# Band attention values: from half-bank pieces spread over the head pairs to full-bank products at the band's entry, with a spill

## The chip, the cores and the metric

The kernel runs on one core of a Trainium2 chip. The metric is the device time of one execution in microseconds (us), here the median of several. TensorE (PE) multiplies matrices; its weight loads (PEld) overlap its matmuls. VectorE (DVE), ScalarE (ACT) and GpSimd (POOL) work elementwise; SyncE (SP) issues the transfers between the chip's DRAM and its on-chip memory, in the order of its queue. Matmul results land in PSUM, in banks of 128 x 512 f32.

## The reference, cut to what matters

The network has two layers, each a mixer and a SwiGLU feed-forward, over 1024 tokens and 1024 channels. The change touches the second mixer, chunked band attention with 16 heads of 64:

```python
def chunk_band_mixer(u, w_qkv, rel_bias, w_out):
    qkv = (u @ w_qkv).reshape(bsz, n_chunks, CHUNK, 3, C_HEADS, C_DIM)
    q, k, v = qkv[:, :, :, 0], qkv[:, :, :, 1], qkv[:, :, :, 2]
    ...
    scores = scores + bias.astype(jnp.float32)[None, None]
    p = jax.nn.softmax(jnp.where(valid[None, :, None, None, :], scores, -jnp.inf), axis=-1).astype(v.dtype)
    parts = [jnp.einsum('bnqhk,bnkhd->bnqhd', p[..., i * CHUNK:(i + 1) * CHUNK], v_p[:, i:i + n_chunks])
             for i in range(LEFT_CHUNKS + 1)]
    o = functools.reduce(jnp.add, parts)
    return o.reshape(bsz, seq, MIX_ODD) @ w_out
```

The values v are `u` (1024 x 1024) times the last 1024 columns of `w_qkv`. Each token attends to its own chunk of 64 and the eight before it.

## The kernel before

**Numbers.** An f32 operand is split into a rounded part (hi) and the rest (lo), and each product takes three matmuls, hi*hi, hi*lo, lo*hi (`mm3`, L286: lines 289, 290, 291). A weight tile of 128 x 512 is loaded into a buffer "wr"; a cast makes "wh" (L252 on ScalarE or L254 on VectorE), a subtraction makes "wl" (L257). There are four buffers of each kind.

**Memory.** Most tiles of 128 x 512 come from one heap of 60 units ("u", `unit`, L186). In the band, the normalized input takes 32 of them (two token halves x eight depth tiles x hi and lo) and the two rows of roots two more. PSUM is dealt out as "mm" (two banks, for projections and values), "z" (two pairs of banks, for scores, maxes and denominators) and "o" (two banks, for outputs).

**Order.** The framework's planner places the instructions on the engines: it goes by the order in which the program issues them, but where the next one isn't ready by its own estimates it takes a later one that is. On the chip each engine then keeps the order it was given. The feed-forward parts are pinned to program order; the band is not.

**The band** (`mixer1`, L1309). Heads go in eight pairs of 128 columns. At the entry come the values of pairs 0 and 1 (`vgen(0, [0, 1])`, L1319), the queries and keys of pair 0 (`band_project`, L1143) and the row maxes of its first token half. Then for each pair p, `weave` (L798) issues attention steps and, between them, work for the next pair in proportion to given costs: the projection of pair p+1 (2 weights x 2 halves x 8 depth tiles x 3 = 96 matmuls of 512 columns) and, for p < 6, the values of group p // 2 + 1 (two pairs, 256 columns) for token half p % 2. So the values' weights of the later groups are loaded and split twice, once for each half. Pair 6 has half of pair 7's projection as filler, and pair 7 the other half and the output projection.

`values` (L811) computes for each block of 128 tokens, with the input block as the stationary operand and 256 weight columns as the moving one; two blocks share a PSUM bank. `put_values` (L830) scales 128 x 128 pieces out of PSUM into units (L838).

An attention step (`band_attend`, L1198) is: scores into z (L1214, L1215), bias add on VectorE (L1216), exponential on ScalarE (L1217), running sum of exponentials on GpSimd (L1085), and some steps later the weighted sum of values (`weighted`, L840, line 844), four steps' sums issued together. `band_max` (L1174) computes scores (L1188), adds the bias and takes row maxes (L1191), and transposes them through TensorE (L1046) once for each pair and token half. `soft_finish` (L1097) makes the denominators (L1101) and stores the output tile (L1113). In `band_project`, L1152 scales the projection, L252, L257 and L1161 split it into units.

Of the kernel before, what the change touches and what calls it, by code (L numbers as in the profile page):

```python
# [10 lines left out]
F32 = mybir.dt.float32  # L11
F32R = mybir.dt.float32r
# [4 lines left out]
P = 128  # L17
S = 1024
D = 1024
KD = D // P  # L20
HALF = 512
# [137 lines left out]
class Trunk:  # L159
# [651 lines left out]
    def values(self, wsrc, s, kper, nk, ng, vts, hfs):  # L811
# [6 lines left out]
        for b0 in range(4 * hfs[0], 4 * hfs[-1] + 4, per):  # L818
# [8 lines left out]
                    yield 3 * MM_US * ncol / HALF  # L827
            self.put_values(s, ps, b0, ncol, vts)

    def put_values(self, s, ps, b0, ncol, vts):  # L830

        for g in range(ncol // P):
            if b0 % 4 == 0:
                vts[g].append(self.unit(F32, (P, 4, P)))
            for b in range(b0, b0 + HALF // ncol):
                hf, r = divmod(b, 4)
                v, q = vts[g][hf][:, r, :], ps[:, (b - b0) * ncol + g * P:][:, :P]
                self.nc.scalar.activation(v, q, AF.Identity, scale=s.rc[hf][:, r:r + 1])  # L838
# [470 lines left out]
    def mixer1(self, u, h_d, h2_d):  # L1309
        a = self.a  # L1310
        o_d = self.spill("o1_")
        out = Stream()
        half = lambda hf, *e: self.out_half(hf, a["w_out1"], o_p[hf], lambda hf, m: h_d[hf][m], list(range(KD)), out,
                                            h2_d, *e)
        with self.phase("band", BAND_TEMPS):
            vts = [[] for _ in range(8)]
            vgen = lambda g, hf: self.values([a["w_v1"][2 * g], a["w_v1"][2 * g + 1]], u, 4, KD, 1,
                                             vts[2 * g:2 * g + 2], hf)
            self.now(vgen(0, [0, 1]))  # L1319
            new = lambda: ([[], []], [[], []])  # L1320
            proj = new()
            self.now(self.band_project(0, u, proj))
            tq, tk = self.band_bias(0, "bias_q"), self.band_bias(0, "bias_k")
            self.now(self.band_max(0, proj, tq))
            for p in range(8):
                nxt, fill, cost, tqn, tkn = new(), iter(()), 0.0, None, None
                if p < 6:
                    fill = self.chain(self.band_project(p + 1, u, nxt), vgen(p // 2 + 1, [p % 2]))
                    cost = 28.0
                elif p == 6:  # L1330
                    fill, cost = self.band_project(7, u, nxt, [0]), 16.0

                def late(p=p, nxt=nxt):
                    nonlocal tqn, tkn
                    tqn, tkn = self.band_bias(p + 1, "bias_q"), self.band_bias(p + 1, "bias_k")
                    yield from self.band_max(0, nxt, tqn)

                first, second = (self.band_attend(p, hf, proj, tk, vts[p], o_d) for hf in range(2))
                top = self.band_max(1, proj, tq)
                if p < 7:  # L1340
                    self.weave(self.chain(self.with_max(first, top, 1), self.with_max(second, late(), 4)), 6.8,
                               fill, cost)
                else:
                    o_p = [[None] * KD, [None] * KD]
                    first = self.with_max(first, self.out_loads(o_d[0], 7, o_p[0]), 0)
                    second = self.with_max(second, self.out_loads(o_d[1], 7, o_p[1]), 0)
                    fill = self.chain(self.band_project(7, u, proj, [1]), self.free(top))
                    self.weave(self.ending(first), 2.5, fill, 8.0)
                    o_p[0][7] = o_d[0][7]
                    self.weave(self.ending(second), 5.0, half(0), 41.5)  # L1350
                    o_p[1][7] = o_d[1][7]
                proj, tq, tk = nxt, tqn, tkn
        return out, half(1, 1)
# [53 lines left out]
def _ktiles(w, cols):  # L1407
    w = w[:, cols]
    kt = w.shape[0] // P
    return np.ascontiguousarray(w.reshape(kt, P, w.shape[1]).transpose(1, 0, 2)).reshape(P, -1)  # L1410


def _mtiles(w, m=P):
    return np.stack([_ktiles(w, np.arange(i, i + m)) for i in range(0, w.shape[1], m)])


def _layout(i):
    out = {}
# [4 lines left out]
    w = i["ev_w_in"][0]  # L1423
    c = [np.arange(t * P, t * P + P) for t in range(5)]
# [6 lines left out]
    vt = []  # L1431
    for g in range(2):
        t = _ktiles(w, vb + np.arange(g * 256, g * 256 + 256))
        vt += [t[:, :1024], t[:, 1024:]]
    out["w_vb"] = np.ascontiguousarray(np.stack(vt))
    w = i["ev_w_uq"][0]
    uq = []
    for h in range(8):
        b = 96 * h
# [3 lines left out]
    w = i["ev_w_ukv"][0]  # L1443
# [4 lines left out]
    w = i["od_w_qkv"][0]  # L1448
    out["w_qk1"] = np.stack([_ktiles(w, o + np.arange(p * P, p * P + P)) for p in range(8) for o in (0, 1024)])
    vt = []  # L1450
    for g in range(4):
        t = _ktiles(w, 2048 + np.arange(g * 256, g * 256 + 256))
        vt += [t[:, :1024], t[:, 1024:]]
    out["w_v1"] = np.ascontiguousarray(np.stack(vt))
    out["w_out1"] = _mtiles(i["od_w_out"][0])
    out["w_gate"] = np.stack([_mtiles(i["w_gate"][l]) for l in range(2)])
# [1 line left out]
    w = np.stack([_mtiles(i["w_down"][l]) for l in range(2)])  # L1458
# [4 lines left out]
    w = w.reshape(w.shape[:3] + (FT, P))[:, :, :, order]  # L1463
    out["w_down"] = np.ascontiguousarray(w).reshape(w.shape[:3] + (FT * P,))
    rb = i["od_rel_bias"][0]
    s = np.arange(P)[:, None]
# [36 lines left out]
```

## Time and profile before

| what | value |
|---|---|
| times of three runs | 2551.01, 2552.98, 2554.29 us |
| median | 2552.98 us |
| profiled execution, its time | 2553.58 us |
| its span, first to last instruction | 2551.9 us |
| mean granted TensorE clock | 0.995 |
| values' evictions (L838) in the band | 64, from 1332.8 to 1717.5 us |
| band's score and max work | about 1373 to 1840 us |

A busy row counts the union of an engine's instructions. Matmuls overlap in a pipeline, so that one's duration is longer than the distance from its start to the next one's; the distance is what a stream costs. A row of windows gives the length, then busy time and count of each engine, the granted clock, the share of the DMA engines and GB/s. A row of groups gives line, engine, operation, tiles, shapes and count, then busy time and mean ns, then idle time before and what ended it. A row of waits gives who waited for whom, total, times and longest. A row of the timeline gives start and duration.

### The profile page before, as it was taken

The numbers are of one execution on the slowest core, as the hardware profiler recorded it, in microseconds if no ns is written. First come the engines' busy times: TensorE is split into PE (matmuls) and PEld (weight loads), VectorE is DVE, ScalarE is ACT, GpSimd is POOL, SyncE is SP. The second block draws the span as 40 slices with busy tenths as digits, with TensorE's granted clock in tenths as the row PEclk, the third lists the DMA queues.
The fourth block names the chain that finished last, engine by engine and source line by source line (L and its number), as shares of the span: only waits on it lengthen the run. The fifth ranks groups of instructions, "written<-read, shape, count | busy, mean of one in ns | idle before, by whom it ended". The sixth has DMA issues, their size and how long they took to land.

```text
span 2551.9 us, 33625 instructions
## 1 busy us (share of the span) xinstructions
PE 2478.1 (97%) x11710; PEld 1938.4 (76%) x11710; DVE 1858.1 (73%) x3072; ACT 1152.1 (45%) x1996; POOL 493.8 (19%) x475
## 2 busy tenths in 40 slices
PE   9999989999999999999999999999999999999997
PEld 7776766557778888888888777776777888888886
DVE  7988796565886666677766777777788676667775
ACT  5777565344454434433353443334445443443324
POOL 0333335652000000000031334345200000000004
PEclk9999999999999999999999999999999999999998
DMA  5222102125434334476652222223633433447661
GB/s 155 54 65 64 41 26 60 54 84 165 153 124 149 120 128 145 149 259 211 227 167 69 79 87 75 75 93 98 190 128 128 148 130 118 145 156 261 217 208 71
DMA packets 182250, 323.91 MB, mean 127 GB/s; under 512 B 21312, under 2 KB 37568, under 8 KB 182080
## 3 DMA queue, kind: packets, MB, share of 16 engines
q1 hardware_dynamic: 182080, 321.76, 38.0%
q8 instruction: 93, 1.52, 0.2%
q14 instruction: 77, 0.63, 0.1%
HBM read 222.58 MB, written 84.41 MB: 120 GB/s over the span
## 4 chain that ended last, share of the span: by engine, by line
PE 74%; DVE 8%; DMA 1%; ACT 1%; issue 1%; POOL 0%; DVEq 0%; SPq 0%; ACTq 0%; POOLq 0%
PE z L76 25%; PE mm L76 13%; PE o L76 7%; PE mm L289 6%; PE mm L290 6%; PE mm L291 6%; PE o L844 4%; DVE u L76 2%; PE z L1214 1%; PE z L1188 1%; PE z L1215 1%; PE z L1133 1%; DVE u L312 1%; PE z L1101 1%; PE z L1134 1%
## 5 line engine op out<-in xcount | busy, mean ns | idle before, releaser
L76 PE MATMUL z<-u,wh 128*128 128x512 f32 x976 | 302.3, 390 | 6.5 <-DVE u L76 6.5
L76 PE MATMUL z<-u,vh 128*128 128x512 f32 x976 | 301.8, 390 | 2.8 <-DVE u L76 2.8
L289 PE MATMUL mm<-u,wh 128*128 128x512 f32 x720 | 287.8, 400 | 3.5 <-DVE f L1003 1.4
L290 PE MATMUL mm<-u,wh 128*128 128x512 f32 x720 | 283.8, 394 | 0.0
L291 PE MATMUL mm<-u,wl 128*128 128x512 f32 x720 | 282.4, 393 | 0.0
L257 POOL TENSOR_TENSOR wl<-wr,wh 128x512 fp32r<-128x512 f32 (+2 forms) x95 | 122.0, 1289 | 803.3 <-ACT wh L252 736.0
L76 PE MATMUL mm<-u,wh 128*128 128x512 f32 x720 | 223.4, 392 | 4.6 <-ACT wh L76 4.6
L76 PEld LDWEIGHTS z<-u,wh 128*128 128x128 f32 x976 | 183.2, 188 | 47.5 <-DVE u L76 9.5
L76 PEld LDWEIGHTS z<-u,vh 128*128 128x128 f32 x976 | 182.9, 188 | 43.1 <-ACT u L76 4.4
L76 PE MATMUL z<-u,wl 128*128 128x512 f32 x488 | 190.0, 389 | 1.4 <-DVE wl L76 1.4
L76 PE MATMUL z<-u,vl 128*128 128x512 f32 x488 | 189.9, 389 | 0.0
L289 PEld LDWEIGHTS mm<-u,wh 128*128 128x128 f32 x720 | 135.4, 188 | 54.7 <-issue 27.6
L76 PEld LDWEIGHTS mm<-u,wh 128*128 128x128 f32 x720 | 134.7, 188 | 35.6 <-ACT wh L76 6.9
L290 PEld LDWEIGHTS mm<-u,wh 128*128 128x128 f32 x720 | 135.5, 188 | 27.2 <-issue 3.2
L291 PEld LDWEIGHTS mm<-u,wl 128*128 128x128 f32 x720 | 135.3, 188 | 27.3 <-issue 0.9
L844 PE MATMUL o<-a,u 128*64 128x512 f32 (+3 forms) x768 | 154.6, 474 | 0.0
L76 PE MATMUL mm<-u,vh 128*128 128x512 f32 x496 | 152.7, 389 | 0.0
L76 PE MATMUL mm<-u,wl 128*128 128x512 f32 x360 | 140.8, 391 | 0.8 <-DVE wl L76 0.5
L257 POOL TENSOR_TENSOR u<-wr,u 128x512 fp32r<-128x512 f32 x8 | 10.9, 1374 | 669.5 <-ACT u L252 669.5
L1085 POOL TENSOR_TENSOR b<-b,a 128x512 f32<-128x512 f32 (+3 forms) x80 | 110.1, 1377 | 125.8 <-ACT a L1217 104.1
L1216 DVE TENSOR_TENSOR a<-z,bias 128x1024 f32<-128x1024 f32 (+3 forms) x96 | 78.2, 823 | 76.9 <-PE z L1215 71.0
L76 ACT CAST vh<-vr 128x512 fp32r<-128x512 f32 (+1 forms) x166 | 96.1, 579 | 82.5 <-DVE vr L76 31.5
(244 smaller groups left out, 5859.4 us busy)
## 6 DMA issues: line engine op xcount, KB each, us to landing
u<-f_t SPq DMA_DIRECT2D x144, 256.0 KB, 5.0
vr<-in_w_up SPq DMA_DIRECT2D x88, 256.0 KB, 4.4
wr<-in_w_gate SPq DMA_DIRECT2D x88, 256.0 KB, 3.7
f_t<-x SPq DMA_DIRECT2D x72, 256.0 KB, 2.0
wr<-in_w_out SPq DMA_DIRECT2D x64, 256.0 KB, 3.1
f_t<-e SPq DMA_DIRECT2D x54, 256.0 KB, 3.6
ld<-f SPq DMA_DIRECT2D x54, 256.0 KB, 5.1
u<-u SPq DMA_DIRECT2D x96, 128.0 KB, 2.2
```

What stands on the lines that cost most here:

```text
L76: return lambda *a, **k: self.tc.keep_in_program_order(f(*a, **k))
L257: self.eng(eng).tensor_tensor(lo, src, hi.bitcast(F32), ALU.subtract)
L289: mm(out, wh, xh, start=first, stop=False, skip_group_check=onto)
L290: mm(out, wh, xl, start=False, stop=False, skip_group_check=onto)
L291: mm(out, wl, xh, start=False, stop=last, skip_group_check=onto)
L312: self.eng(eng).tensor_tensor(acc, acc, sq, ALU.add)
L844: self.nc.tensor.matmul(o[rh, cs], vt[j // 4][:, j % 4, rh], w[:, e, cs], start=first, stop=last)
L1085: self.eng("dve" if dest[2] else "pool").tensor_tensor(st["esum"][:, :, cs], old[:, :, cs], ex[:, :, cs], ALU.add)
L1101: nc.tensor.matmul(den[64 * e:64 * e + 64, :], self.ones[:, 0:64], esum[:, e, :], start=True, stop=True)
L1133: mm(z[:, e, cs], kth[0:kr, bs], qh[0:kr, cs], start=True, stop=False)
L1134: mm(z[:, e, cs], kth[0:96, bs], ql[0:96, cs], start=False, stop=False)
L1216: nc.vector.tensor_tensor(ex[:, :, cs], z[:, :, cs], tk[:, :, xs], ALU.add)
```

## The change

`wide_values` takes the place of `values` in the band. It takes 512 columns (four pairs) at a time: it loads and splits the eight weight tiles once, into 16 heap units, and for each token half and block of 128 tokens fills one PSUM bank with 8 x 3 matmuls of 512 columns. Both groups run at the band's entry. `put_away` keeps the values of pairs 0 and 1; those of pairs 2 to 7 are written to DRAM (12 tiles of 256 KB). `back(p + 1)` reads two tiles back at the start of pair p, for p from 1 to 6. The filler of pairs 0 to 5 is the projection alone, with a cost of 23 in place of 28. The weights' layout follows.

```diff
+    def wide_values(self, g, s, out):
+
+        wraw = [self.raws(self.a["w_v1"][4 * g + i]) for i in range(4)]
+        ws = []
+        for raws in wraw:
+            for r in raws:
+                hi, lo = self.unit(F32R), self.unit(F32R)
+                self.split(r, hi, lo, "act", "dve")
+                ws.append((hi, lo))
+        vts = [[] for _ in range(4)]
+        for hf in range(2):
+            for r in range(4):
+                ts = slice(r * P, (r + 1) * P)
+                ps = self.bank()
+                for k in range(KD):
+                    self.mm3(ps, s.u[hf][0][k][:, ts], s.u[hf][1][k][:, ts], *ws[k], k == 0, k == KD - 1)
+                self.put_values(s, ps, 4 * hf + r, HALF, vts)
+            for i, v in enumerate(vts):
+                out(4 * g + i, hf, v[hf])
+
...
             vts = [[] for _ in range(8)]
-            vgen = lambda g, hf: self.values([a["w_v1"][2 * g], a["w_v1"][2 * g + 1]], u, 4, KD, 1,
-                                             vts[2 * g:2 * g + 2], hf)
-            self.now(vgen(0, [0, 1]))
+            v_d = [[self.dp.tile([P, HALF], F32, name=f"v{p}_{hf}") for hf in range(2)] for p in range(8)]
+
+            def put_away(p, hf, v):
+                if p < 2:
+                    vts[p].append(v)
+                else:
+                    self.nc.sync.dma_start(v_d[p][hf], v.rearrange("p a b -> p (a b)"))
+
+            def back(p):
+                for hf in range(2):
+                    v = self.unit(F32, (P, 4, P))
+                    self.nc.sync.dma_start(v.rearrange("p a b -> p (a b)"), v_d[p][hf])
+                    vts[p].append(v)
+
+            for g in range(2):
+                self.wide_values(g, u, put_away)
...
             for p in range(8):
                 nxt, fill, cost, tqn, tkn = new(), iter(()), 0.0, None, None
+                if p and p < 7:
+                    back(p + 1)
                 if p < 6:
-                    fill = self.chain(self.band_project(p + 1, u, nxt), vgen(p // 2 + 1, [p % 2]))
-                    cost = 28.0
+                    fill, cost = self.band_project(p + 1, u, nxt), 23.0
...
     vt = []
-    for g in range(4):
-        t = _ktiles(w, 2048 + np.arange(g * 256, g * 256 + 256))
-        vt += [t[:, :1024], t[:, 1024:]]
+    for g in range(2):
+        t = _ktiles(w, 2048 + np.arange(g * HALF, (g + 1) * HALF))
+        vt += [t[:, c:c + 1024] for c in range(0, 4 * 1024, 1024)]
```

## The prediction

> **What bounds the kernel.** First the page: its engine line, the granted clock by slices and the chain that ended last.
>
> ```profile
> PE 2478.1 (97%) x11710; PEld 1938.4 (76%) x11710; DVE 1858.1 (73%) x3072; ACT 1152.1 (45%) x1996; POOL 493.8 (19%) x475
> ...
> PEclk9999999999999999999999999999999999999998
> ...
> PE 74%; DVE 8%; DMA 1%; ACT 1%; issue 1%; POOL 0%; DVEq 0%; SPq 0%; ACTq 0%; POOLq 0%
> ```
>
> TensorE is busy nearly always, at full clock, and carries 74% of the chain. So time is won where TensorE gets less to do, and lost where its queue has less to do while it waits. Next the band alone, the only stage that the change touches: busy time by windows. The first window is the band's entry (pair group 0 of the values); the others run from the start of one pair's first max transpose (L1046) to that of the next: pairs 4, 5 and 6.
>
> ```profile
> core 0: us, PE busy (x) PEld busy (x) DVE busy (x) ACT busy (x) POOL busy (x), PEclk, DMA share, GB/s
> 1326.03:1351.10 25.07, 25.07 (x203) 24.41 (x202) 9.40 (x16) 6.63 (x17) 0.00 (x0) 1.00 0.15 49
> ...
> 1603.38:1660.63 57.25, 55.95 (x324) 43.54 (x325) 42.33 (x92) 23.49 (x41) 22.13 (x23) 1.00 0.26 79
> 1660.63:1717.88 57.25, 55.97 (x324) 43.55 (x325) 42.28 (x92) 23.50 (x41) 22.15 (x23) 1.00 0.24 78
> 1717.88:1767.16 49.28, 49.27 (x232) 31.07 (x232) 38.36 (x88) 21.20 (x35) 29.74 (x27) 1.00 0.35 110
> ```
>
> A pair takes 57.25 us with TensorE busy 55.97; VectorE is busy 42.28 (74%). Transfers are at a quarter. The waits of TensorE between 1320 and 1840 us are these:
>
> ```profile
> PE z L1214 <- DVE a L1216: 7.3, 6, 1.2
> PE z L1188 <- DVE m L1191: 0.5, 1, 0.5
> PE z L1046 <- DVE maxes L1044: 0.5, 1, 0.5
> ```
>
> One wait of 1.2 us in each of six pairs; all else is matmul after matmul.
>
> **The change, part by part.** *The matmuls.* Values now take 768 matmuls of 256 columns: 8 token blocks x 8 depth tiles x 3 products x 4 groups, 192 at entry and 96 in each of pairs 0 to 5. They become 384 of 512 columns (2 groups), all at entry. The spacing is read from starts in the timeline of TensorE: values at entry (every third matmul is L290), and pair 0's projection (every third is L289).
>
> ```profile
> 1336.11 0.28 PE L290 MATMUL mm<-wl,u 128*128 128x256 f32 x1
> ...
> 1340.06 0.28 PE L290 MATMUL mm<-wl,u 128*128 128x256 f32 x1
> ```
>
> ```profile
> 1352.49 0.39 PE L289 MATMUL mm<-u,wh 128*128 128x512 f32 x1
> ...
> 1372.21 0.39 PE L289 MATMUL mm<-u,wh 128*128 128x512 f32 x1
> ```
>
> The first pair of rows stands 33 matmuls apart: 3.95/33 = 0.1197 us each. The second stands 87 apart: 19.72/87 = 0.2267. Removed: 768 x 0.1197 = 91.9 us (23.0 at entry, 11.5 in each of six pairs). Added: 384 x 0.2267 = 87.0. Net **-4.9 us** if TensorE's sum decides. The durations in the rows (0.28 and 0.39) are pipelined and would overstate it. The Trainium skill ("TensorE: Matmul & The Clock Gate", section "Back-to-back issue gap") gives a warm spacing of N/2.4 ns plus 2.5 ns, that is 109.2 and 215.8 ns. By it 384 merged pairs would save only 1.0 us; the rows show 119.7 and 226.7, and the rows decide.
>
> *The splits, evictions and transfers.* What leaves a pair, from the groups of pair 4 and the issues of 1380 to 1720 us, with the nearest rows for what comes:
>
> ```profile
> L257 DVE TENSOR_TENSOR wl<-wr,wh 128x512 fp32r<-128x512 f32 x4 | 3.1, 769 | 0.1
> ...
> L252 ACT CAST wh<-wr 128x512 fp32r<-128x512 f32 x4 | 2.5, 617 | 2.1 <-PE mm L290 1.7 <-POOL b L1085 0.4
> L838 ACT ACTIVATE u<-mm,rc 128x128 f32<-128x128 f32 x8 | 2.4, 364 | 2.2 <-PE z L1214 1.5 <-PE mm L291 0.7
> ```
>
> ```profile
> wr<-in_w_v SPq DMA_DIRECT2D x20, 256.0 KB, 2.9
> ...
> o<-f SPq DMA_DIRECT2D x11, 256.0 KB, 2.0
> ld<-o SPq DMA_DIRECT2D x4, 256.0 KB, 3.0
> ```
>
> Each of six pairs loses 4 casts (2.5 us of ScalarE), 4 rests (3.1 of VectorE), 8 evictions (2.4 of ScalarE) and 4 weight loads; the entry gains 12 tiles to split (16 for 4, 28 to 16 overall) and the 48 evictions. At entry VectorE is busy 9.4 of 25 us, and the longer entry (25 + 64 us) takes 12 x 0.77 = 9.2 of it: hidden behind 87 us of matmuls, except at its start. There the first product needs tile 0 and each next tile 3 x 0.2267 = 0.68 us later, about one rest. The loads can begin during the last feed-forward matmuls. The heap has 60 units: 32 operands, 2 roots, 16 split weights and 8 values make 58, so the second group's weights must wait for the first group's to be freed, tile by tile during its last token block (24 x 0.2267 = 5.4 us). If that cover fails, a late tile costs one load, cast and rest, 2.9 + 0.62 + 0.77 = 4.3 us, at each group: 0 to 8.6 us. I take 0, since the freed tile comes 5.4 us before its successor is needed.
>
> Spills: 12 writes of 256 KB (2.0 us by the nearest row), no reader waits for the write but the later reload. Reloads: two per pair from pair 1 to 6 for the pair after, 3.0 us by the nearest row, with a whole pair as cover. On SP they stand ahead of projection weights and bias of that pair; a reload that waits for a free unit holds those. Bounds: 0, and 3.0 x 6 = 18 us if each stood bare; I take 0, since two transfers replace four.
>
> *What the pairs lose as cover.* A pair falls to 57.25 - 11.5 = 45.8 us by TensorE's sum, and VectorE to 42.3 - 3.1 = 39.2 of it, 86% instead of 74%. The values were filler between the attention's steps. Pair 6 already runs with little filler (half a projection), and shows what happens. Weighted sums (L844) by windows, then projections (L290, one matmul in three), for pair 5's two halves and pair 6's:
>
> ```profile
> 1660.63:1685.11 24.48, 1.73 (x16) 0.99 (x16) 1.00 0.30 94
> 1685.11:1717.88 32.77, 5.39 (x32) 2.12 (x32) 1.00 0.20 66
> 1717.88:1742.35 24.47, 4.96 (x32) 2.42 (x32) 1.00 0.33 100
> 1742.35:1767.16 24.81, 8.57 (x32) 2.17 (x32) 1.00 0.38 120
> ```
>
> ```profile
> 1717.88:1742.35 24.47, 6.74 (x17) 3.20 (x17) 1.00 0.33 100
> 1742.35:1767.16 24.81, 4.50 (x11) 2.07 (x11) 1.00 0.38 120
> ```
>
> Pair 6's window holds 28 x 3 = 84 projection matmuls (36 of them pulled forward from pair 7) and 64 weighted ones. Pair 5's 45.8 us without values holds 96 and 48. So pair 6 should take 45.8 - 12 x 0.2267 + 1.73 = 44.8; it takes 49.28, 4.5 more. The weighted sums say where: 13.53 us for 64, against 7.12 + 1.73 = 8.85. They are cut up:
>
> ```profile
> 1708.11 3.01 PE L844 MATMUL o<-a,u 128*64 128x512 f32 x16
> ```
>
> ```profile
> 1747.54 1.02 PE L844 MATMUL o<-a,u 128*64 128x512 f32 x2
> ```
>
> Sixteen together take 3.0 us in pair 5; two alone take 1.0 in pair 6, where the planner, out of filler, issues each as it becomes ready. The price is bounded by 4.5 us a pair above and by the present wait below (-1.2, if it goes). Filler decides: pair 6 has 48 projections of its own and pays all; the present pairs have 96 and 96 half ones, as good as 144, and pay nothing; after the change they have 96, midway. So I take half, 2.3, x 6 = **+13.8 us**.
>
> Sum: 2553.58 (profiled execution; 1.7 around its span of 2551.9) - 4.9 + 13.8 = **2562.5 us**, 0.4% over it. That execution stands 0.6 above the median shown.
>
> **The rivals.** *TensorE's sum holds.* Projections alone keep the groups whole: 2548.7. For it: nothing but six short waits is seen in TensorE's queue now, and VectorE at 86% still has room. Against: pair 6.
>
> *The six waits go too* (faster). The timeline of pair 1 shows what VectorE did ahead of one:
>
> ```profile
> 1469.06 0.99 DVE L257 TENSOR_TENSOR wl<-wr,wh 128x512 fp32r<-128x512 f32 x1
> ...
> 1470.80 0.69 DVE L1216 TENSOR_TENSOR a<-z,bias 128x512 f32<-128x512 f32 x1
> ```
>
> The rest of a values tile, 0.99 us, delays the bias add, and behind that the adds which free the score bank. Gone, it frees most of each 1.2 us: -7.3 in all, 2541.4. The Trainium skill ("Perfetto Trace Analysis", section "Optimization Strategy") reads the same gap repeated on the saturated engine as too little buffer space; here the score banks are two, and the six equal waits agree. Against it: the matmuls which the values gave TensorE in that stretch go as well, and the wait then grows.
>
> *Cut as in pair 6* (slower): 6 x 4.5 - 4.9 = +22.1, 2575.7. It decides as soon as a pair's own projections are used up before its second group of weighted sums. For it, the L290 row of pair 5's first half:
>
> ```profile
> 1660.63:1685.11 24.48, 9.10 (x23) 4.33 (x23) 1.00 0.30 94
> ```
>
> 23 x 3 = 69 of the 96 projections are drawn there already, which leaves 27 for the second half, where pair 6 used 33 and still cut its sums. Against it: that haste is in part the planner filling time which the values would otherwise fill.
>
> *The entry starves* on weights: up to +8.6 - 4.9, 2557.3. *The planner does not do as said*, and the matmuls mingle as before: no change, 2553.
>
> **How the numbers follow.** Chances: half price 0.40 (2562.5), sum holds 0.17, waits go 0.15, full price 0.15, entry 0.08, not as said 0.05. About 0.2% (5.1 us) is what a measurement of this kernel can tell from no change. Sum-holds lies on that edge and is halved; of the half price, its cheap end (under 1.6 us a pair, 0.08) is within. Faster: 0.085 + 0.15 = 0.235, say 0.24; within: 0.085 + 0.08 + half the entry case 0.04 + 0.05 = 0.255, say 0.26; slower: 0.50. Range: 2541 (waits gone) to 2584 (full price and starved entry, 2575.7 + 8.6). The likeliest case alone spans 2555 to 2570.
>
> **What would show it.** Entry: 384 matmuls of 512 columns at 0.227 us, some 87 us without a wait; a wait at tile 0 or between groups proves the entry case. Pairs 0 to 5: period between L1046 marks 45.8 (sum holds), 44.6 (waits gone), about 48 (forecast), over 50 (full price). Weighted sums per pair in more than three groups and over 7.1 us prove the cutting; new waits with groups whole would prove VectorE the bound instead. Reloads land long before use. Wrong altogether if another stage moves.

## The result, and the profile after

| | before, beside it | after |
|---|---|---|
| median | 2553.64 us (2551.01 to 2554.72) | 2573.11 us (2571.95 to 2573.9) |
| profiled execution, its span | 2551.9 us | 2572.2 us |
| mean granted TensorE clock | 0.995 | 0.991 |

The ratio is 1.0074 (95% interval 1.0058 to 1.009): the change makes the kernel slower by 19.5 us, a little more than twice what was forecast (8.9, to 2562.5). In the experiments below one execution of even filler took 4885.81 us, and its median leaves it out. Lines of the band below 830 keep their numbers; later ones stand 20 higher (L844 is now L864, L1046 L1066, L1188 L1208, L1214 L1234, L1216 L1236). The page's engine line of the kernel after:

```profile
PE 2492.3 (97%) x11326; PEld 1923.9 (75%) x11326; DVE 1849.7 (72%) x3060; ACT 1140.8 (44%) x1984; POOL 493.1 (19%) x475
```

TensorE has 384 instructions fewer and is still busy longer. So the time has to be sought stage by stage. Marks are the starts of the first max transpose of each pair (L1046, L1066) in TensorE's timeline; the entry runs from the last feed-forward product (1325.80 before, 1327.39 after) to the first mark.

| stretch | before | after | difference |
|---|---|---|---|
| up to the last feed-forward product | 1325.80 | 1327.39 | +1.6 |
| entry | 53.61 | 125.98 | +72.4 |
| pair 0 | 52.08 | 46.65 | -5.4 |
| pairs 1 to 5 | 286.39 | 239.61 | -46.8 |
| pair 6 | 49.28 | 48.18 | -1.1 |
| pair 7 and all behind it | 784.74 | 784.39 | -0.3 |

By TensorE's sum the entry should have grown by 384 x 0.2267 - 192 x 0.1197 = 64.1 us; it grew by 8.3 more. Each of pairs 0 to 5 should have shrunk by 11.5, 68.9 in all, and pair 6 not at all; they shrank by 53.3, so 15.6 are missing there. The 1.6 us ahead of the entry are within the scatter: in thirteen of the fourteen kernels of this study, all with the same feed-forward part, the last norm product but one (L322) starts anywhere from 1304.13 to 1308.00 (the fourteenth, unread products, comes later at 1318.90 and is taken up at the end). The sum: -4.9 + 8.3 + 15.6 + 1.6 - 0.3 = 20.3, which is the whole difference of the spans.

Busy time by windows: the first four cut the entry's start, the fifth is the rest of it, then comes pair 5.

```profile
core 0: us, PE busy (x) PEld busy (x) DVE busy (x) ACT busy (x) POOL busy (x), PEclk, DMA share, GB/s
1327.40:1330.90 3.50, 0.38 (x2) 0.00 (x0) 2.70 (x5) 1.24 (x2) 0.00 (x0) 1.00 0.23 88
1330.90:1334.00 3.10, 1.13 (x2) 0.30 (x2) 1.07 (x2) 1.86 (x4) 0.00 (x0) 0.78 0.00 0
1334.00:1337.00 3.00, 2.98 (x7) 2.14 (x8) 3.00 (x6) 1.52 (x3) 0.00 (x0) 0.50 0.25 86
1337.00:1340.00 3.00, 3.00 (x13) 2.06 (x11) 0.32 (x1) 1.24 (x2) 0.00 (x0) 0.59 0.63 176
1340.00:1453.37 113.37, 113.37 (x501) 93.10 (x502) 26.53 (x55) 30.86 (x86) 7.12 (x8) 1.00 0.25 82
1691.84:1739.63 47.79, 46.37 (x228) 32.17 (x229) 39.28 (x89) 18.51 (x29) 22.10 (x22) 1.00 0.27 84
```

The entry's loss lies all at its start: 6.6 us in which TensorE is busy for 1.5, and then a stretch at half clock, 7 matmuls in 3 us where 13 would fit. From 1340 on there is no hole, not where the second group's weights follow the first group's either. TensorE's own timeline there, then ScalarE's:

```profile
1327.39 0.39 PE L291 MATMUL mm<-u,wl 128*128 128x512 f32 x1
1330.94 1.13 PE L322 MATMUL o<-u,ones 128*128 128x512 f32 x2 [3.17 <-DVE u L312]
1334.02 1.22 PE L289 MATMUL mm<-u,u 128*128 128x512 f32 x2 [1.95 <-ACT u L252]
...
1335.57 0.63 PE L291 MATMUL mm<-u,u 128*128 128x512 f32 x1
1335.99 0.63 PE L289 MATMUL mm<-u,u 128*128 128x512 f32 x1
```

```profile
1332.83 0.63 ACT L326 ACTIVATE u<-u 128x512 f32<-128x512 f32 x1
1333.36 2.16 ACT L252 CAST u<-wr 128x512 fp32r<-128x512 f32 x4
```

The casts of the value weights (now "u<-wr", into heap units) begin only at 1333.36, straight after the last step of the feed-forward's norm (L326) and without a wait of their own, so it is their place in ScalarE's queue that held them. Yet the loads of four weight tiles had been issued long before, as SyncE's queue shows:

```profile
1307.94 4.53 SPq L273 DMA_DIRECT2D wr<-in_w_v  x2
...
1318.78 0.33 SPq L273 DMA_DIRECT2D wr<-in_w_v  x1
...
1334.95 10.99 SPq L273 DMA_DIRECT2D wr<-in_w_v  x8
```

In the kernel before, value products filled TensorE's queue while the norm's last product waited for VectorE, and its timeline there shows no wait:

```profile
1329.62 0.28 PE L289 MATMUL mm<-wh,u 128*128 128x256 f32 x1
1329.74 1.02 PE L322 MATMUL o<-u,ones 128*128 128x512 f32 x2
```

After the change nothing stands there, so TensorE sees that 3.2 us wait bare, then 2 us for the first cast, then the half clock.

In the pairs, TensorE's largest wait in total from 1320 to 1880 us, and the weighted sums of pair 5 by halves:

```profile
PE z L1234 <- DVE a L1236: 6.9, 6, 1.6
```

```profile
1691.84:1714.04 22.20, 1.74 (x16) 0.99 (x16) 1.00 0.24 78
1714.04:1739.63 25.59, 6.45 (x32) 2.62 (x32) 1.00 0.30 90
```

The wait for the bias add is still there once a pair, though the rests of the values' weights have left VectorE. The sums of pair 5 take 8.19 us instead of 7.12, so of the 2 us that a pair misses, about 1.1 are cut sums. Hardly any of the rest is new waiting: TensorE is idle for 47.79 - 46.37 = 1.42 us of pair 5, and was for 57.25 - 55.97 = 1.28 before. The rest is in the busy time of other products, which are cut too: the eight of the denominators (L1101, now L1121) take 2.69 us in pair 5 instead of 2.06.

### The profile page after: what moved, and what is told of

Its sections match the earlier page's. It is cut to its first block, busy times and chain, and to the rows that moved or that the text cites. A ratio compares the mean times of both kernels' runs of the same rounds, so it can differ in the third digit from the quotient of the medians.

```text
span 2572.2 us, 32870 instructions
## 1 busy us (share of the span) xinstructions
PE 2492.3 (97%) x11326; PEld 1923.9 (75%) x11326; DVE 1849.7 (72%) x3060; ACT 1140.8 (44%) x1984; POOL 493.1 (19%) x475
## 4 chain that ended last, share of the span: by engine, by line
PE 72%; DVE 9%; ACT 2%; DMA 2%; issue 1%; SPq 0%; DVEq 0%; POOL 0%; ACTq 0%
PE z L76 24%; PE mm L76 12%; PE o L76 6%; PE mm L289 6%; PE mm L290 6%; PE mm L291 6%; PE o L864 3%; DVE u L76 2%; PE z L1208 1%; PE z L1234 1%; PE z L1235 1%; DVE u L312 1%; PE z L1153 1%; PE z L1121 1%; DMA wr<-in_w_down 1%
## 5 line engine op out<-in xcount | busy, mean ns | idle before, releaser
L76 PE MATMUL z<-u,wh 128*128 128x512 f32 x976 | 302.5, 390 | 6.5 <-DVE u L76 6.5
L76 PE MATMUL z<-u,vh 128*128 128x512 f32 x976 | 303.8, 393 | 3.7 <-DVE u L76 3.7
L76 PE MATMUL mm<-u,wh 128*128 128x512 f32 x720 | 223.5, 392 | 4.5 <-ACT wh L76 4.5
L76 PEld LDWEIGHTS z<-u,wh 128*128 128x128 f32 x976 | 183.3, 188 | 47.2 <-DVE u L76 9.5
L76 PEld LDWEIGHTS z<-u,vh 128*128 128x128 f32 x976 | 184.4, 189 | 44.6 <-ACT u L76 5.2
L76 PE MATMUL z<-u,vl 128*128 128x512 f32 x488 | 190.9, 391 | 0.0
L76 PE MATMUL z<-u,wl 128*128 128x512 f32 x488 | 190.1, 390 | 0.0
L864 PE MATMUL o<-a,u 128*64 128x512 f32 (+3 forms) x768 | 161.5, 475 | 0.0
L76 PEld LDWEIGHTS mm<-u,wh 128*128 128x128 f32 x720 | 134.7, 188 | 35.6 <-ACT wh L76 6.9
L76 PE MATMUL mm<-u,vh 128*128 128x512 f32 x496 | 152.7, 389 | 0.0
L76 PE MATMUL mm<-u,wl 128*128 128x512 f32 x360 | 140.8, 391 | 0.8 <-DVE wl L76 0.5
L76 ACT CAST vh<-vr 128x512 fp32r<-128x512 f32 (+1 forms) x166 | 95.9, 578 | 82.7 <-DVE vr L76 30.7
L76 DVE TENSOR_TENSOR wl<-wr,wh 128x512 fp32r<-128x512 f32 (+1 forms) x190 | 122.6, 651 | 3.2 <-ACT wh L76 3.2
L76 ACT CAST wh<-wr 128x512 fp32r<-128x512 f32 (+1 forms) x190 | 109.5, 583 | 34.0 <-DVE wr L76 28.9
```

The costliest lines, as they stand in the source:

```text
L76: return lambda *a, **k: self.tc.keep_in_program_order(f(*a, **k))
L864: self.nc.tensor.matmul(o[rh, cs], vt[j // 4][:, j % 4, rh], w[:, e, cs], start=first, stop=last)
```

## The experiments

The table gathers them: median, ratio to the kernel before on the same chip with its 95% interval, the first mark, and the distance from each mark to the next pair's.

| kernel | median us | ratio | first mark | pair 0 | pairs 1 to 5 | pair 6 |
|---|---|---|---|---|---|---|
| before | 2553.64 | | 1379.41 | 52.08 | 57.25 to 57.32 | 49.28 |
| after | 2573.11 | 1.0074 (1.0058 to 1.009) | 1453.37 | 46.65 | 47.77 to 48.43 | 48.18 |
| weights apart | 2561.4 | 1.0032 (1.0022 to 1.0041) | 1442.99 | 45.24 | 47.77 to 47.85 | 48.16 |
| no spill | 2571.28 | 1.0064 (1.0049 to 1.0079) | 1453.02 | 46.66 | 47.75 to 47.84 | 48.14 |
| narrow products | 2577.01 | 1.0089 (1.0073 to 1.0106) | 1461.15 | 46.50 | 47.77 to 49.33 | 48.16 |
| even filler | 2574.97 | 1.0081 (1.0064 to 1.0098) | 1454.50 | 46.27 | 48.73 to 49.05 | 48.78 |
| early filler | 2553.97 | 1.0 (0.9991 to 1.001) | 1443.38 | 44.58 | 46.78 to 46.94 | 48.97 |
| unread products | 2615.28 | 1.0239 (1.0221 to 1.0258) | 1458.31 | 50.14 | 52.88 to 52.96 | 48.12 |
| unread again | 2592.29 | 1.0146 (1.0132 to 1.0161) | 1445.04 | 50.12 | 52.85 to 52.91 | 48.14 |
| written order | 2646.24 | 1.0364 (1.0345 to 1.0383) | 1446.06 | 57.94 | 61.55 to 64.44 | 48.19 |
| before, sooner | 2553.57 | 0.9999 (0.9991 to 1.0008) | 1380.55 | 52.88 | 57.12 to 57.16 | 48.28 |
| half wide | 2569.7 | 1.0065 (1.0053 to 1.0078) | 1399.64 | 51.81 | 55.26 to 58.52 | 48.30 |
| wide filler | 2570.21 | 1.0072 (1.0059 to 1.0086) | 1400.51 | 53.53 | 46.93 to 64.04 | 48.97 |
| earlier still | 2560.0 | 1.0029 (1.0017 to 1.004) | 1442.84 | 45.55 | 47.20 to 47.53 | 50.42 |

**Weights apart.** The first group's split weights come from other buffers than the heap.

```diff
-                hi, lo = self.unit(F32R), self.unit(F32R)
+                if g == 0 and len(ws) < 4:
+                    hi, lo = self.wtile(0, "h", F32R), self.wtile(0, "l", F32R)
+                elif g == 0:
+                    t = self.tmp("a", F32R, (P, 1024))
+                    hi, lo = t[:, :HALF], t[:, HALF:]
+                else:
+                    hi, lo = self.unit(F32R), self.unit(F32R)
```

> The changed kernel, but the first group's eight weight tiles are split into buffers of their own (four into the weight buffers, four into score buffers that are idle at the entry) in place of 16 heap units. Theory (the entry starves because the split tiles wait for heap units, behind the last feed-forward work, and the idle stretch then halves the TensorE clock): the 5.2 us of idle time between the last feed-forward matmul and the first value matmul and the stretch at clock 0.5 vanish, entry from there to the first max transpose 126 us to about 118, time 2573 to 2564 to 2567. Rival (the weights' loads or VectorE are late by themselves): the idle time stays, 2573.

It takes 11.7 us off the median. TensorE's timeline, ScalarE's and the same windows of this kernel:

```profile
1327.96 0.39 PE L289 MATMUL mm<-a,u 128*128 128x512 f32 x1
...
1329.80 1.02 PE L322 MATMUL o<-u,ones 128*128 128x512 f32 x2
```

```profile
1317.10 0.62 ACT L252 CAST wh<-wr 128x512 fp32r<-128x512 f32 x1 [0.56 <-issue]
```

```profile
1327.40:1330.90 3.50, 3.50 (x16) 2.45 (x15) 2.86 (x6) 1.70 (x4) 0.00 (x0) 1.00 0.85 255
1330.90:1334.00 3.10, 3.07 (x14) 2.21 (x13) 2.83 (x5) 2.42 (x6) 0.00 (x0) 1.00 0.63 211
```

The first cast is 16 us earlier, the norm's product finds value products around it, and the clock stays at 1.00. So it was the heap as the home of the split weights that starved the entry; whether units were really lacking, or the planner only reckoned them so, is not told apart. The entry, from the last feed-forward product (1325.01 here) to the first mark, takes 118.0 us instead of 126.0, which is TensorE's sum (53.61 + 64.1 = 117.7) to 0.3. Pair 0 is 1.4 us shorter, with a clock of 1.00 where it had a stretch at half clock. The other pairs did not change, but for the one of 48.43. So some 9.4 of the 11.7 us are the edit's; another 2.4 us lie ahead of the entry, in the scatter, and may be why the time came out below the 2564 to 2567 that were expected.

**No spill.** Neither writes nor reloads; pairs 2 to 7 are computed with the values of pairs 0 and 1.

```diff
-                else:
-                    self.nc.sync.dma_start(v_d[p][hf], v.rearrange("p a b -> p (a b)"))
...
-                    back(p + 1)
+                    vts[p + 1] = vts[p - 1]
```

> The changed kernel without the 12 writes and 12 reloads: pairs 2 to 7 take the values of pairs 0 and 1, so the attention of six pairs is computed with other values. Theory (transfers are hidden): within 2 us of 2573, pair period 47.8. Rival (the spill costs, by queue places on SyncE, heap units or DMA): 2568 or less, the pair period towards 45.8.

The pairs keep their length to 0.1 us, but for one of 48.43 that is 47.8 here. The spill is hidden.

**Narrow products.** Every product of 512 columns at the entry is cut into two of 256.

```diff
-                    self.mm3(ps, ..., *ws[k], k == 0, k == KD - 1)
+                    for b in range(2):
+                        cs = slice(256 * b, 256 * b + 256)
+                        self.mm3(ps[:, cs], ..., ws[k][0][:, cs], ws[k][1][:, cs],
+                                 k == 0 and b == 0, k == KD - 1 and b == 1)
```

> The changed kernel with each value matmul of 512 columns cut into two of 256 (768 in all, as before the change, all at the entry). Theory (merging saves 4.9 us at the rows' spacings of 0.1197 and 0.2267): 2573 + 5 = 2578, less up to 1 where an entry wait is filled. Rival (the merge saves only 1 us): 2574.

It costs 3.9 us by the medians, but the two kernels' intervals overlap, and in the profiled execution, the longest of the four (2580.3), the half clock lasted longer too. The spacing in its trace, once the clock is whole again, says it more sharply:

```profile
1379.83 0.28 PE L291 MATMUL mm<-u,u 128*128 128x256 f32 x1
...
1385.95 0.28 PE L291 MATMUL mm<-u,u 128*128 128x256 f32 x1
```

These stand 51 products apart, 6.12/51 = 0.1200 us each, and two of them less one of 512 columns (0.2267), 384 times, is 5.1 us. The merge itself is worth about what was reckoned.

**Even filler.** The cost of the projections goes from 23 to 18.8, so that a tenth of them is left for after the last step of the pair, as in the kernel before.

```diff
-                    fill, cost = self.band_project(p + 1, u, nxt), 23.0
+                    fill, cost = self.band_project(p + 1, u, nxt), 18.8
```

> The changed kernel with the weave cost of pairs 0 to 5 at 18.8 in place of 23, so that the projection is issued evenly to the end of each pair's attention. Theory A (the weighted sums are cut up because the pair's own filler is spent too early, and that is half of the 2.1 us a pair above TensorE's sum): sums in fewer groups, pair period 47.8 to about 47, time 2568. Theory B (the pace is set by score banks and VectorE whatever the order): pair period within 0.3 of 47.8, time 2573.

Both expectations missed: pairs 1 to 5 are 0.6 to 1.0 us longer, so filler that stands later is worse. The total shows less of it, because the stages behind the pairs, which the edit does not touch, took 781.40 us in this profile instead of 784.38.

**Early filler.** The weights-apart kernel with a cost of 28, which issues the filler sooner.

```diff
-                    fill, cost = self.band_project(p + 1, u, nxt), 23.0
+                    fill, cost = self.band_project(p + 1, u, nxt), 28.0
```

> The weights-apart kernel with the filler's cost at 28 instead of 23, so that the next pair's 96 projections are all issued by about three quarters of a pair. Theory A (it is the place of the filler that decides: a stretch of a pair without projections has its weighted sums cut and its waits bare): the second half of each pair runs bare, pairs 1 to 5 go from 47.8 to 49 us or more, total 2566 to 2572. Rival B (only the amount of filler counts, wherever it stands): pairs stay at 47.8 within 0.3, total 2561 within 2.

Both expectations missed: pairs became 1.0 us shorter than in weights apart, and the kernel is level with the one before. One pair by windows, then TensorE's largest wait in total from 1320 to 1840 us, then the weighted sums of the next pair by halves:

```profile
1581.55:1628.34 46.79, 46.44 (x228) 32.13 (x229) 37.47 (x88) 18.75 (x29) 21.98 (x22) 1.00 0.29 90
```

```profile
PE z L1214 <- DVE m L1217: 2.4, 8, 0.5
```

```profile
1628.34:1650.25 21.91, 1.73 (x16) 0.99 (x16) 1.00 0.22 64
1650.25:1675.18 24.93, 6.89 (x32) 2.12 (x32) 1.00 0.33 98
```

The wait for the bias add is gone from every pair, and TensorE's idle time falls by about the 1.0 us that a pair gained. The sums are cut more (8.62 us against 8.19), but the denominators are whole again (2.06 us). The level total owes as much to the stages behind the pairs: pair 6 ends 3.9 us later than in the kernel before (1771.09 against 1767.16), and what follows takes 780.69 us here and 784.70 there, though the edit does not touch it. All other kernels but the two with unread products stand between these two there.

**Unread products.** The weights-apart kernel with 32 more matmuls in each of pairs 0 to 5.

```diff
+    def unread(self, s):
+        ps = self.bank()
+        for i in range(2):
+            for k in range(KD):
+                for x in range(2):
+                    self.nc.tensor.matmul(ps, s.u[0][0][k][:, :P], s.u[i][x][k], ...)
+                yield 2 * MM_US
+        t = self.sp.tile([P, 1], F32, tag="unread", name=self.nm("unread"))
+        self.nc.scalar.copy(t, ps[:, 0:1])
...
+                    fill, cost = self.chain(self.band_project(p + 1, u, nxt), self.unread(u)), 30.7
```

> The weights-apart kernel with 32 more matmuls of 512 columns per pair in pairs 0 to 5, on tiles that are there anyway, into one bank that nobody reads but one small copy: filler and nothing else, 32 x 0.2267 = 7.25 us of TensorE per pair. It computes them beside the kernel's own work. Theory A (a pair loses about 2.1 us for want of filler, and gets it back with filler): pairs 1 to 5 take 45.8 + 7.25 = 53.1 us, 5.2 over the 47.8 of the weights-apart kernel; total about 2561 + 6 x 5.2 = 2592. Rival B (the 2.1 us are a fixed cost, filler adds its full time): 55.0 us a pair, total about 2604. Rival C (VectorE or the score banks bound the pair, matmuls have room): pairs of 51 or less, total below 2580.

The pairs took what theory A said, 52.9 us, but the total was 23 us over it, because stages that the edit does not touch were longer. So it was run again without the new small tile.

```diff
-        t = self.sp.tile([P, 1], F32, tag="unread", name=self.nm("unread"))
+        m2 = self.sp.tile([P, 2, 4, 2], F32, tag="m2", name=self.nm("m2"))
```

> The kernel of the unread products again, with the one column that is copied out put into a small tile that exists anyway instead of a new one; nothing else differs. There the pairs took 52.9 us as theory A said, but stages that the edit does not touch were longer too (the band's first mark came 15 us later). Theory P (the new small tile moved the buffers behind it, and the place of the buffers costs time everywhere): without it the first mark is back at 1443 us, pairs stay at 52.9, total 2561.4 + 30.5 = 2592. Rival Q (the products themselves do it, by the planner's order or otherwise): 2615 again.

2592.29, on the expected 2592. A pair by windows, and its weighted sums:

```profile
1600.90:1653.76 52.86, 52.16 (x260) 37.65 (x261) 39.39 (x88) 19.12 (x30) 22.43 (x22) 1.00 0.27 82
```

```profile
1600.90:1624.51 23.61, 1.74 (x16) 0.99 (x16) 1.00 0.21 65
1624.51:1653.76 29.25, 5.39 (x32) 2.12 (x32) 1.00 0.31 96
```

7.25 us of matmuls lengthen a pair by 5.1. The sums are back at 7.12 and the denominators at 2.06, to the hundredth as before the change, and TensorE is idle for 0.7 us instead of 1.4. Without the 7.25 us the pair would stand at 45.6, where TensorE's sum is 45.8. This is the plainest sign that the pairs lost cover.

**Written order.** The weights-apart kernel with TensorE's instructions of pairs 0 to 5 in the order of the program.

```diff
+                if p < 6:
+                    self.nc = PinnedCore(self.tc)
+                    self.nc.sync, self.nc.vector, self.nc.scalar, self.nc.gpsimd = nc.sync, nc.vector, nc.scalar, nc.gpsimd
```

> The weights-apart kernel with TensorE's instructions of pairs 0 to 5 kept in the order the program issues them, so that each four steps' weighted sums stand together. Theory A1 (the 2.1 us come from the planner's cutting of the sums): pairs of 46 to 47 us, total 2550 to 2557. Rival A2 (the cuts are the planner's answer to operands that come late; in the written order TensorE waits for them instead): pairs of 49 us or more with waits of over 1 us ahead of scores or sums in the trace, total over 2568.

A1 fell, A2 held. TensorE's waits from 1446 to 1820 us (pinned instructions all carry L76), and a pair by windows:

```profile
PE z L76 <- DVE maxes L1070: 20.7, 11, 1.9
PE z L76 <- DVE a L1242: 19.3, 20, 1.7
```

```profile
1566.48:1629.85 63.37, 53.89 (x228) 37.58 (x229) 40.44 (x88) 18.83 (x29) 21.77 (x22) 0.85 0.23 69
```

With the cuts forbidden TensorE waits for the maxes and the bias add, up to 1.9 us at a time, so the cuts are the planner's answer to operands that come late. Forbidding them costs 14 to 17 us in each of pairs 1 to 5, part of it at a clock of 0.85.

**Before, sooner.** The kernel before with 31 for 28, the values still in the pairs.

```diff
-                    cost = 28.0
+                    cost = 31.0
```

> The kernel before with one number changed: the filler's cost in pairs 0 to 5 is 31 instead of 28, so that projections and values end with the pair instead of a tenth of them being left for after the last step. Theory A (the wait of 1.2 us in each pair comes from filler that stands too late; the early filler took it away in the kernel with wide values): the waits for the bias add go, pairs take about 56 us, total 2553 - 7 = 2546. Rival R (the rest of a values tile on VectorE, L257, stands ahead of the bias add wherever the filler is): waits stay, 2553 within 3. Rival S (second half of a pair runs short of filler): pairs over 57.5, 2556 or more.

No change in the total. TensorE's waits from 1320 to 1840 us and the weighted sums of pair 5 by halves:

```profile
PE z L1188 <- DVE m L1191: 0.6, 1, 0.6
PE z L1046 <- DVE maxes L1044: 0.5, 1, 0.5
```

```profile
1661.99:1686.21 24.22, 1.51 (x10) 0.96 (x10) 1.00 0.27 83
1686.21:1719.11 32.90, 6.69 (x38) 2.51 (x38) 1.00 0.25 77
```

All six waits of 1.2 us went, with the rests of the values still on VectorE; the sums went from 7.12 to 8.20 us. What a wait gave back, the cuts took: 57.12 against 57.25. Theory A had the waits right and the time wrong, rival R the reverse. So in this kernel the wait was not worth its 1.2 us, while early filler, which took the same wait out of the weights-apart kernel, did gain about its length.

**Half wide.** Pairs 0 to 3 wide at the entry, pairs 4 to 7 narrow as filler.

```diff
-            for g in range(2):
-                self.wide_values(g, u, put_away)
+            self.wide_values(0, u, put_away)
+            vgen = lambda g, qs: self.values([a["w_v1"][2 * g], a["w_v1"][2 * g + 1]], u, 4, KD, 1,
+                                             vts[2 * g:2 * g + 2], None, [2 * q for q in qs])
...
-                    fill, cost = self.band_project(p + 1, u, nxt), 23.0
+                    vs = vgen(2, [p]) if p < 4 else vgen(3, [2 * p - 8, 2 * p - 7])
+                    fill, cost = self.chain(self.band_project(p + 1, u, nxt), vs), 29.0 if p < 4 else 34.5
```

> Only pairs 0 to 3 have their values from 512 columns at the entry (split weights kept apart from the heap, pairs 2 and 3 spilled); those of pairs 4 to 7 stay in pieces of 256 columns as filler, 48 matmuls in each of pairs 0 to 3 (cost 29) and 96 in pairs 4 and 5 (cost 34.5). Theory A (filler enough keeps the pair at TensorE's sum): pairs 0 to 3 take 45.8 + 48 x 0.1197 = 51.5 us, pairs 4 and 5 57.25 or a little less, the entry 43.5 us of values instead of 46.0; total 2553 - 2.5 = 2550.5, and less by 1.1 for each wait that goes. Rival B (each pair has some 2 us of fixed waiting whatever fills it): pairs 0 to 3 take 53.5, total about 2559.

Pair 0 took 51.8 as theory A said; the others did not (55.3 to 58.5), and the total lies above both theories. VectorE in pair 3, then TensorE, then two windows behind it:

```profile
1605.06 2.72 DVE L257 TENSOR_TENSOR u<-t,u 64x512 fp32r<-64x512 f32 x2
1607.81 0.30 DVE L1217 CUSTOM_DVE_ANT_0 z<-z,bias 128x128 f32<-128x128 f32 x1
```

```profile
1608.22 0.80 PE L1214 MATMUL z<-u,u 128*128 128x256 f32 x2 [2.19 <-DVE m L1217]
```

```profile
1605.50:1608.60 3.10, 0.91 (x6) 0.71 (x4) 3.04 (x5) 0.00 (x0) 2.96 (x4) 0.94 0.22 79
1608.60:1612.00 3.40, 3.40 (x11) 1.25 (x12) 1.74 (x6) 1.88 (x5) 3.26 (x5) 0.55 0.65 210
```

Two rests of the next pair's projection stand ahead of the max work on VectorE, TensorE waits 2.2 us for the score bank, and 3.4 us at about half clock follow. Filler alone does not secure the pace; at this place, where the long VectorE operations fall decided as well. No run moved them away.

**Wide filler.** Built on weights apart as half wide is, but pairs 4 to 7 too come from 512 columns, in pairs 0 to 3, with the rests on GpSimd.

```diff
+    def wide_pieces(self, g, s, blocks, vts, out):
+        ps = [self.bank() for _ in blocks]
+        for i in range(4):
+            w = self.weight(self.a["w_v1"][4 * g + i])
+            for k in (2 * i, 2 * i + 1):
+                for n, b in enumerate(blocks):
...
+                    yield 3 * MM_US
+        for n, b in enumerate(blocks):
+            self.put_values(s, ps[n], b, HALF, vts)
+            if b % 4 == 3:
+                for i, v in enumerate(vts):
+                    out(4 * g + i, b // 4, v[b // 4])
```

> Pairs 0 to 3 have their values from 512 columns at the entry, as in the half-wide kernel; those of pairs 4 to 7 come from 512 columns too, two token blocks (48 matmuls, 10.9 us) as filler in each of pairs 0 to 3, after the projections, with their weights split anew in each pair and the rests on GpSimd instead of VectorE. Cost 31 in pairs 0 to 3, 28 and no values in pairs 4 and 5. So the merge is whole and four of six pairs keep their filler. Theory A (with filler the pair comes to TensorE's sum, as with the unread products): pairs 0 to 3 take 45.6 + 10.9 = 56.5 us, pairs 4 and 5 46.8, total 2554 (the kernel with the early filler) - 4 x 1.2 = 2549. Rival B (as in the half-wide kernel, splits on VectorE get ahead of the max work): pairs 0 to 3 take over 58 us, with waits of 2 us for the maxes and half clock after them, total 2560 or more.

Pair 2 took 55.79, even less than the 56.5 of theory A, and pair 0 53.53; pairs 1 and 3, in which a half of the values is complete and is spilled, took 64. The total is in rival B's range, but not by its cause, since the rests of the values' weights run on GpSimd. ScalarE and VectorE in pair 1, then TensorE:

```profile
1512.46 1.26 ACT L252 CAST u<-t 64x512 fp32r<-64x512 f32 x2 [4.70 <-DMA v<-u]
```

```profile
1513.11 1.41 DVE L257 TENSOR_TENSOR u<-t,u 64x512 fp32r<-64x512 f32 x2 [2.50 <-ACT u L252]
```

```profile
1515.51 0.73 PE L1232 MATMUL z<-u,u 128*128 128x512 f32 x2 [2.99 <-DVE a L1260]
```

The cast waits 4.70 us for a heap unit until the spill has been written, VectorE waits for the cast, and the score bank is not freed. The writes that cost nothing after the change cost here, where a cast needs the unit at once.

**Earlier still.** The weights-apart kernel with a cost of 32.

```diff
-                    fill, cost = self.band_project(p + 1, u, nxt), 23.0
+                    fill, cost = self.band_project(p + 1, u, nxt), 32.0
```

> The weights-apart kernel with the filler's cost at 32; 23 gave pairs of 47.8 us, 28 gave 46.8 and 2554. Theory A (the sooner the projections stand, the fewer waits are left; the bare sums cost less than the waits did): 46.0 a pair, total 2550. Rival B (28 has taken the waits already, and what is left is the bare second half, which grows): 47 us or more a pair, total 2555 or more.

47.2 to 47.5 a pair: rival B. Of the four costs tried (18.8 on the kernel after, the others with weights apart) 28 was the best, and no kernel that was run beats the one before; early filler ties with it.

## Why the prediction was right or wrong

**The sign and the merge were right.** Narrow products cost 3.9 us by the medians and 5.1 by their spacing, where 4.9 were reckoned. The formula of the Trainium skill ("TensorE: Matmul & The Clock Gate", section "Back-to-back issue gap", which states it for the isolated gap of a matmul) would have given 1.0; the spacings measured here, 0.1200 and 0.2267, differ from it and decide. The measured time lies within the range, but above the 2555 to 2570 that the likeliest case alone was given.

**The cover was right, in mechanism and nearly in size.** The forecast was 2.3 us in each of six pairs and a period of about 48; the periods of pairs 1 to 5 are 47.8 but for one, a loss of 2.1 each. That the pairs lose 15.6 in all against 13.8 is in part luck, for the two ends were not foreseen: pair 0 loses 6.1 (52.08 - 11.5 is 40.6, it took 46.65), of which 1.4 go with its stretch at half clock, and pair 6 gains 1.1. Why pair 0 loses so much more was not followed. Unread products bring the lost cover back: 45.6 and whole sums. The prediction spoke of cut sums only. They are half of the 2 us; the other half is other products cut as well, the denominators' above all, and only 0.14 us is new idle time. Half of the bound was a guess between two cases, and so luck in its size; the three costs 18.8, 23 and 28 (48.8, 47.8, 46.8 us) show that the place of the filler counts beside its amount.

**The step that failed is the entry's starvation, taken at 0.** Its ground was that "the loads can begin during the last feed-forward matmuls" and that "the freed tile comes 5.4 us before its successor is needed". The loads did begin in time, and the change from the first group to the second did cost nothing. But the split tiles are heap units, and their casts began only behind the feed-forward's last norm step. The term measured 8.3 us at the entry. That this is near the upper bound of 8.6 is chance, since it came by another way than the one priced there: 3.2 us of a wait that value products had covered, 2 us for the first cast, and the rest mostly the half clock. Weights apart, which removes it, gains 8.0 at the entry and 1.4 in pair 0 (11.7 by the medians). The prediction looked for what the new step waits for, and not for what the old step at that place had covered.

**The spill at 0 was right**: without it the pairs keep their length to 0.1 us, all but one.

**The rivals.** "The six waits go too" read the wait as the work of a rest of a values tile on VectorE. Both halves of that fell: after the change the rests are gone and the wait stays (6.9 us in six pairs), and in the kernel before with earlier filler the rests stay and the wait goes. Nor was the wait worth its length there, since the sums were cut instead. The Trainium skill's reading ("Perfetto Trace Analysis", section "Optimization Strategy"), a repeated gap as a possible sign of too little buffer space, was not tried: no kernel had a third pair of score banks. But the gap went in two kernels with the same two pairs, by the place of the filler alone. "Cut as in pair 6" asked 4.5 us a pair, and pairs 1 to 5 lost 2.1. "The entry starves" was right, and held beside the forecast, not in its place: 2562.5 + 8.3 is 2570.8, and the scatter ahead of the band and the rest of the cover make up the difference to 2573.11.

## What to carry to other kernels

When work is moved out of a place, ask what it covered there, at its old place and at its new neighbour: here value products had covered a norm's wait at the entry and, in six pairs, attention operands that come late, and that cost about five times what larger matmuls saved (8.3 + 15.6 against 4.9 us). The home of a buffer is part of a schedule: tiles from a shared heap were not written before the phase ahead had finished, the same tiles elsewhere were. And price a wait by removing it, not by its length: the same wait was worth nothing in the kernel before and about its length in the weights-apart kernel.

## What was not expected of the hardware

**The clock halves after short waits, not always.** After the change 3.2 and 2 us of waiting were followed by matmuls 0.43 us apart and a clock of 0.50. But in pair 0 a wait of 1.6 us was enough:

```profile
1494.76 0.33 PE L1234 MATMUL z<-u,u 128*128 128x128 f32 x1 [1.61 <-DVE a L1236]
```

```profile
1497.00:1499.50 2.50, 2.50 (x7) 1.95 (x6) 1.45 (x5) 0.00 (x0) 0.59 (x1) 0.50 0.85 274
```

The same wait in the same pair of the weights-apart kernel, 1.63 us in the first of these windows and behind the same matmuls, left the clock whole:

```profile
1482.00:1484.50 2.50, 0.87 (x5) 0.39 (x4) 2.47 (x3) 0.21 (x2) 1.05 (x1) 1.00 0.58 201
1484.50:1487.00 2.50, 2.26 (x11) 1.74 (x12) 1.92 (x7) 0.91 (x2) 1.79 (x2) 1.00 0.41 106
```

In the wide filler kernel, too, two waits of about 3 us had different ends: the one quoted there (2.99 us, from 1512) left the clock whole, another (3.15 us, from 1630) was followed by half clock.

```profile
1515.50:1518.90 3.40, 3.38 (x14) 2.38 (x15) 2.53 (x8) 0.40 (x1) 1.03 (x2) 1.00 0.77 268
...
1633.70:1637.10 3.40, 3.22 (x8) 2.55 (x9) 2.08 (x8) 0.46 (x2) 1.57 (x2) 0.51 0.86 305
```

The Trainium skill ("TensorE: Matmul & The Clock Gate", section "Part 1: The HAM clock gate (the "warmup" mystery)") says that the clock falls to half after an idle window of about 3.4 us, and that the windows run freely, without regard to the kernel. The free running fits equal waits with different ends; the length does not fit the 1.6 us, beside which only another 0.24 us of waiting stands. So a wait of 1.6 us was followed by about 3 us at half rate, which cost about as much again.

**A tile of four bytes a partition moved 23 us.** Unread products and unread again differ only in a small tile with a tag of its own, ahead of the stages' buffers: 2615.28 against 2592.29. The first of these windows is from the former, the second from the latter, both long before the edit:

```profile
500.00:1000.00 500.00, 489.89 (x2109) 375.96 (x2109) 342.17 (x520) 210.98 (x366) 58.84 (x43) 0.99 0.39 128
```

```profile
500.00:1000.00 500.00, 489.37 (x2139) 380.47 (x2137) 346.87 (x527) 214.74 (x373) 58.46 (x42) 0.99 0.39 130
```

At the same clock TensorE gets through 30 matmuls fewer in 500 us. It is not waiting more: from 1050 to 1070 us, busy all 20 us at a clock of 1.00 in both, it has 88 matmuls in the former and 90 in the latter, so the products themselves stand farther apart. That the buffers behind the small tile should stand elsewhere is the only difference known; no run shows their places, and by what they would cost time was not tried.
